# Mixer of a hybrid attention and GLA layer: two heads side by side on halves of TensorE's array, softmax steps over two heads

## The chip, the core and the metric

The kernel runs on one core of a Trainium2 chip. The metric is the device time of one execution in microseconds (us), the median of several runs. A trace of one more execution shows every instruction: on TensorE (PE for matmuls, PEld for loads of the stationary operand), VectorE (DVE), ScalarE (ACT), GpSimd (POOL), and the DMA transfers, which SyncE (SP) issues.

## What is computed

The reference is two layers of a diffusion backbone over 256 tokens of width 1024, with 256 context tokens. The change lies in the mixer of the first layer. It has two branches, whose outputs are laid side by side and projected: windowed attention with 8 query heads on 2 key heads (width 64), and gated linear attention (GLA) in both directions with 4 heads (keys 64 wide, values 128) in chunks of 64 tokens. All of it is float32. Cut to what matters:

```python
def window_attention(q, k, v, kc, vc, sink):
    s_band = jnp.einsum('bnigrd,bnjgd->bgrnij', qb, kb).astype(jnp.float32) * scale
    s_ctx = jnp.einsum('bnigrd,blgd->bgrnil', qb, kc).astype(jnp.float32) * scale
    s_band = jnp.where(valid, s_band, -jnp.inf)
    p = jax.nn.softmax(jnp.concatenate([s_band, s_ctx, sink_l], axis=-1), axis=-1)
    o = (jnp.einsum('bgrnij,bnjgd->bnigrd', p[..., :nk].astype(vb.dtype), vb)
         + jnp.einsum('bgrnil,blgd->bnigrd', p[..., nk:nk + L].astype(vc.dtype), vc))
...
def gla_chunked(q, k, v, log_a, s0):
    q_t = qc_ * jnp.exp(g)
    k_t = kc_ * jnp.exp(-g)
    att = jnp.where(lower, jnp.einsum('bnihd,bnjhd->bnhij', q_t, k_t), 0.0)
    o = jnp.einsum('bnhij,bnjhv->bnihv', att, vc_)
    ...
    o = o + jnp.einsum('bnihd,bnhdv->bnihv', q_t, s_prev)
```

## The kernel before

The program runs in stages, one after the other: the first feed-forward block over tokens and context (two streams), the mixer, a feed-forward block, and the second layer (feed-forward, pooling mixer, feed-forward, final norm). Weights come from HBM through four buffers in `weight` (L138); each is split into a rounded part `hi` on ScalarE (L144) and the rest `lo` on VectorE (L145), and `product` (L322) multiplies a 1024-deep block of weights with the operand in 24 matmuls (L327 to L329).

In the mixer (L705) the projections come one 128-wide block at a time (`project`, L749, in the order of `ORDER`). Small tasks hang on them: rotation of queries and keys (`rope`, L794), transposition of values (`values`, L786), the decay factors of GLA (`gate`, L822), the output gate (`output_gate`, L811). On their results work:

- `scores` (L967): the products of GLA's keys and queries, four heads a block of 128 tokens. `q_t` holds each head in a tile of its own whose other 64 partitions are zero, so that a matmul over all 128 rows (L971) gives one head. A masked copy (L973) writes `att`.
- `states` (L944): the running states `S` of GLA; its matmuls (L951) write the column halves 0 to 63 and 64 to 127 in turn, for two heads.
- `gla_head` (L977): for a head, `att` times values (L984, L991) and `S` times queries (L989) into one bank, then a norm (from L998) with its own small product (L999).
- `attend` (L898): for one query head (j, g) and one block qb of 128 queries: the scores over 256 tokens and 256 context tokens (L904; `k_g` holds each key head with 64 zero partitions), mask and maximum (L907), exponentials (L910, L911), sum and reciprocal (L912, L913), scaling (L914), four transposes (L921), a copy to `PT` (L922), and after the second block the values (L931: four matmuls into one column half of a bank that two heads share). `split` (L892) cuts the result into two parts for the output projection. There are 16 such tasks; three probability buffers (`PBUF`) let three be under way.
- `output` (L1014): the output projection with `merged` (L336, L337), whose first two blocks take up each piece as it is ready.

What is issued when is set by a planner, `Flow` (L63): each task is a generator that gives, step by step, how long TensorE is thought to be busy and what VectorE and ScalarE do after it (`step`, L103); the task of the lowest rank (`RANK`) that is ready by this reckoning is written next. The framework's own scheduler may then shift instructions within an engine. Each engine works through its own list in order; TensorE may start a matmul before earlier ones of another part of its array are through, as the trace shows.

Of the kernel before, what the change touches and what calls it, by code (L numbers as in the profile page):

```python
# [8 lines left out]
F32 = mybir.dt.float32  # L9
# [6 lines left out]
D = 1024  # L16
# [34 lines left out]
PBUF = 3  # L51
# [55 lines left out]
class Body:  # L107
# [597 lines left out]
    def mixer(self, cur, nxt):  # L705
# [12 lines left out]
        k_g = t(lp, [128, 2, 512])  # L718
        k_t = t(lp, [128, 2, 2, T])
        q_t = t(lp, [128, 2, 4, T])  # L720
# [4 lines left out]
        for z in (k_g, q_t, KT):  # L725
            nc.gpsimd.memset(z, 0.0)
# [67 lines left out]
        def rope(blk):  # L794
# [7 lines left out]
            if blk == "ka":  # L802
                for g in (0, 1):
                    r = slice(g * 64, g * 64 + 64)
                    nc.vector.tensor_tensor(k_g[r, g, :T], t1[r], t2[r], op=ALU.add)
                    nc.scalar.copy(k_g[r, g, T:], z[r, T:])
            else:
                nc.vector.tensor_tensor(q_r[:, int(blk[2]), :], t1, t2, op=ALU.add)
# [13 lines left out]
        def gate(d, b):  # L822
# [32 lines left out]
            for hh in (0, 1):  # L855
                r = slice(hh * 64, hh * 64 + 64)
                nc.vector.scalar_tensor_tensor(out=q_t[r, d, 2 * b + hh, :], in0=Z[f"qb{b}"][r], scalar=0.125,
                                               in1=ep[r], op0=ALU.mult, op1=ALU.mult)
# [37 lines left out]
        pv_bank, pv_last, PT = {}, {}, {}  # L896

        def attend(j, g, qb, u):  # L898


            h = g * 4 + j
            sk = self.cols[:, C_SK + h:C_SK + h + 1]
            ps = self.bank()
            nc.tensor.matmul(ps, q_r[:, j, qb * 128:(qb + 1) * 128], k_g[:, g, :], start=True, stop=True)  # L904
            p = t(sp, [128, 512], F32, "P", PBUF)
            st = t(sp, [128, 4], F32, "st", 4)
            nc.vector.tensor_tensor_reduce(out=p, in0=ps, in1=band[:, qb, :], scale=0.125, scalar=sk,  # L907
                                           op0=ALU.add, op1=ALU.max, accum_out=st[:, 0:1])
            nc.vector.tensor_scalar_mul(st[:, 1:2], st[:, 0:1], -1.0)
            nc.scalar.activation(st[:, 3:4], sk, AF.Exp, bias=st[:, 1:2])  # L910
            nc.scalar.activation(p, p, AF.Exp, bias=st[:, 1:2], accum_out=st[:, 2:3])  # L911
            nc.vector.tensor_tensor(st[:, 2:3], st[:, 2:3], st[:, 3:4], op=ALU.add)  # L912
            nc.vector.reciprocal(st[:, 2:3], st[:, 2:3])  # L913
            nc.vector.tensor_scalar_mul(p, p, st[:, 2:3])  # L914
            yield step(0.86, [("D", ATT[0]), ("A", ATT[1]), ("D", ATT[2])])
            if qb == 0:
                PT[h] = t(sp, [128, 4, T], F32, "PT", 2)
            pt = PT[h]
            pk = self.bank()
            for kb in range(4):  # L920
                nc.tensor.transpose(pk[:, kb * 128:(kb + 1) * 128], p[:, kb * 128:(kb + 1) * 128], self.ident)  # L921
            nc.scalar.copy(pt[:, :, qb * 128:(qb + 1) * 128], pk.rearrange("p (k q) -> p k q", q=128))  # L922
            yield step(0.44, [("A", 0.48)], sets=[f"T{u}"])
            if qb == 0:
                return
            if j not in pv_bank:
                pv_bank[j] = self.bank()
            po = pv_bank[j]
            with self.after(pv_last.get(j)):
                for kb in range(4):  # L930
                    ins = nc.tensor.matmul(po[g * 64:(g + 1) * 64, :T], v_sb[:, kb, g * 64:(g + 1) * 64],  # L931
                                           pt[:, kb, :], start=(kb == 0), stop=(kb == 3))
            second = j in pv_last
            pv_last[j] = ins
            if second:
                split(j, po[:, :T])
                yield step(1.72, [("A", 0.31), ("D", 0.34)], sets=[f"a{h}", f"o{j}"])
            else:
                yield step(1.72, sets=[f"a{h}"])
# [27 lines left out]
        def scores(d, tb):  # L967
            ps = self.bank()
            c = slice(tb * 128, (tb + 1) * 128)
            for h in range(4):  # L970
                nc.tensor.matmul(ps[:, h * 128:(h + 1) * 128], k_t[:, d, h // 2, c], q_t[:, d, h, c],  # L971
                                 start=True, stop=True)
            nc.vector.copy_predicated(att[:, d, tb], gm[:, d:d + 1, :].to_broadcast([128, 4, 128]),  # L973
                                      ps.rearrange("p (h i) -> p h i", i=128))
            yield step(0.87, [("D", 0.6)], sets=[f"att{d}{tb}"])

        def gla_head(h):  # L977
            po = self.bank()
            c = slice(h * 128, (h + 1) * 128)
            prev = None  # L980
# [61 lines left out]
        for d in (0, 1):  # L1042
            for tb in (0, 1):
# [244 lines left out]
```

## Time and profile before

| | us |
|---|---|
| three runs | 1159.35, 1162.02, 1163.1 |
| median | 1162.02 |
| the profiled execution | 1161.4 |
| its span, first to last instruction | 1159.2 |
| TensorE busy in the span | 1137.5 |
| VectorE busy | 938.5 |
| ScalarE busy | 587.4 |
| GpSimd busy | 9.9 |

TensorE's clock was granted at 0.997 in the mean. The mixer's scores, states, attention and GLA heads run from about 443 to 546 us of the span; the rest of the output projection follows. Rows of the profile name an instruction by its line in the kernel, its engine, its operation, the tile that it writes and those that it reads, and its shape; `128*64` behind a matmul is the part of the array that it uses (rows times columns). The end of a matmul is modelled, so the distance from one start to the next says more than its busy time. A float32 matmul stands in the trace as two records of a load and a matmul. The order lists of the program count each float32 matmul once.

### The profile page before, as it was taken

To read this page: it belongs to the slowest core of one execution; us is meant where nothing else is said; L and a number is where in the kernel's file an instruction comes from. 1 tells how busy PE (TensorE), PEld (TensorE's weight loads), DVE (VectorE), ACT (ScalarE), POOL (GpSimd) and SP (SyncE) were. 2 spreads that over 40 slices of the span, in tenths; PEclk is the share of its full clock that TensorE was granted. 3 is DMA by queue.
4 is the path that set the end of the run, shared out by engine and by line. 5 is a ranking of instruction groups with operands and counts; after the bars stand their busy time and mean duration, and the time that the engine had idled before them with its cause. 6 is when DMAs were issued, how large, how long until landed. Compare 5 with 4: busy or idle time off the path is not lost.

```text
span 1159.2 us, 19546 instructions
## 1 busy us (share of the span) xinstructions
PE 1137.5 (98%) x7450; PEld 1027.0 (89%) x7450; DVE 938.5 (81%) x1662; ACT 587.4 (51%) x999; POOL 9.9 (1%) x32
## 2 busy tenths in 40 slices
PE   7999999999999999999999999999999999999997
PEld 5899988888888899787999998899999889988886
DVE  6899899787758889776999877989886889967664
ACT  4547645323234474565574444565544556556543
POOL 0000000000000200000000000000000000000000
PEclk9999999999999999999999999999999999999998
DMA  9867557667866535321759977868996864756562
GB/s 332 289 243 240 164 179 233 198 217 243 249 191 191 171 108 177 115 69 54 234 187 324 326 236 246 283 208 284 340 312 203 261 226 147 252 185 192 153 185 88
DMA packets 74544, 247.42 MB, mean 213 GB/s; under 512 B 8273, under 2 KB 8913, under 8 KB 74194
## 3 DMA queue, kind: packets, MB, share of 16 engines
q1 hardware_dynamic: 74450, 246.17, 64.4%
q8 instruction: 58, 0.95, 0.3%
q14 instruction: 36, 0.29, 0.1%
HBM read 245.09 MB, written 1.05 MB: 212 GB/s over the span
## 4 chain that ended last, share of the span: by engine, by line
PE 86%; DVE 7%; DMA 3%; ACT 2%; issue 2%; SPq 0%; DVEq 0%; ACTq 0%
PE t_mm L336 15%; PE t_mm L342 11%; PE t_mm L344 11%; PE t_mm L343 11%; PE t_mm L337 8%; PE t_mm L329 7%; PE t_mm L328 7%; PE t_mm L327 7%; PE t_mm L610 2%; DVE t_lo L145 1%; PE t_mm L931 1%; PE t_mm L904 1%; DVE t_junk L174 1%; DMA t_x<-ctxT 1%; ACT t_hi L144 1%
## 5 line engine op out<-in xcount | busy, mean ns | idle before, releaser
L144 ACT CAST t_hi<-t_raw 128x1024 fp32r<-128x1024 f32 (+1 forms) x344 | 326.0, 950 | 368.2 <-PE t_mm L343 160.8
L145 DVE TENSOR_TENSOR t_lo<-t_raw,t_hi 128x1024 fp32r<-128x1024 f32 (+1 forms) x344 | 376.6, 1097 | 87.2 <-ACT t_hi L144 84.1
L327 PE MATMUL t_mm<-t_xA,t_hi 128*128 128x258 f32 (+1 forms) x912 | 261.0, 287 | 2.7 <-DVE t_x L957 1.6
L329 PE MATMUL t_mm<-t_xA,t_lo 128*128 128x258 f32 (+1 forms) x912 | 259.6, 285 | 3.1 <-DVE t_lo L145 3.1
L328 PE MATMUL t_mm<-t_xA,t_hi 128*128 128x258 f32 (+1 forms) x912 | 258.1, 283 | 0.1
L174 DVE CUSTOM_DVE_ANT_0 t_junk<-t_rawm,t_x 128x1024 bf16<-128x1024 f32 x142 | 181.7, 1280 | 23.8 <-DMA t_rawm<-wmod 22.9
L336 PE MATMUL t_mm<-t_g,t_hi 128*128 128x512 f32 x528 | 186.6, 398 | 0.0
L344 PE MATMUL t_mm<-t_xA,t_lo 128*128 128x256 f32 (+1 forms) x592 | 186.2, 315 | 0.0
L342 PE MATMUL t_mm<-t_xA,t_hi 128*128 128x256 f32 (+1 forms) x592 | 186.2, 315 | 0.0
L343 PE MATMUL t_mm<-t_xA,t_hi 128*128 128x256 f32 (+1 forms) x592 | 186.2, 315 | 0.0
L327 PEld LDWEIGHTS t_mm<-t_xA,t_hi 128*128 128x128 f32 x912 | 173.0, 190 | 5.9 <-DVE t_x L957 1.9
L329 PEld LDWEIGHTS t_mm<-t_xA,t_lo 128*128 128x128 f32 x912 | 172.6, 189 | 4.2 <-DVE t_lo L145 4.2
L328 PEld LDWEIGHTS t_mm<-t_xA,t_hi 128*128 128x128 f32 x912 | 172.7, 189 | 2.4 <-issue 1.4
L337 PE MATMUL t_mm<-t_g,t_lo 128*128 128x256 f32 x528 | 147.9, 280 | 0.0
L336 PEld LDWEIGHTS t_mm<-t_g,t_hi 128*128 128x128 f32 x528 | 99.2, 188 | 23.8
L343 PEld LDWEIGHTS t_mm<-t_xA,t_hi 128*128 128x128 f32 x592 | 112.9, 191 | 6.9
L344 PEld LDWEIGHTS t_mm<-t_xA,t_lo 128*128 128x128 f32 x592 | 112.9, 191 | 6.9
L342 PEld LDWEIGHTS t_mm<-t_xA,t_hi 128*128 128x128 f32 x592 | 112.9, 191 | 6.7
L337 PEld LDWEIGHTS t_mm<-t_g,t_lo 128*128 128x128 f32 x528 | 99.7, 189 | 0.0
L336 PE MATMUL t_mm<-t_xA,t_hi 128*128 128x512 f32 x272 | 95.4, 396 | 0.0
L337 PE MATMUL t_mm<-t_xA,t_lo 128*128 128x256 f32 x272 | 75.4, 278 | 0.0
L342 PE MATMUL t_mm<-t_g,t_hi 128*128 128x512 f32 x176 | 68.5, 389 | 0.0
(244 smaller groups left out, 1388.7 us busy)
## 6 DMA issues: line engine op xcount, KB each, us to landing
t_raw<-wi SPq DMA_DIRECT2D x190, 512.0 KB, 4.6
t_rawm<-wmod SPq DMA_DIRECT2D x118, 512.0 KB, 4.5
t_raw<-wo SPq DMA_DIRECT2D x64, 384.0 KB, 3.6
t_raw<-wo SPq DMA_DIRECT2D x64, 320.0 KB, 3.3
t_raw<-win SPq DMA_DIRECT2D x18, 512.0 KB, 3.7
t_w<-wmod SPq DMA_DIRECT2D x16, 512.0 KB, 6.6
t_raw<-wmod SPq DMA_DIRECT2D x10, 512.0 KB, 4.3
t_raw<-wi0k SPq DMA_DIRECT2D x8, 512.0 KB, 6.3
```

The costliest lines, as they stand in the source:

```text
L144: nc.scalar.copy(hi[:, :n], raw[:, :n])
L145: self.mark = nc.vector.tensor_tensor(lo[:, :n], raw[:, :n], hi.bitcast(F32)[:, :n], op=ALU.subtract)
L174: self.nc.vector.tensor_tensor_reduce(out=junk, in0=w, in1=self.srow[s], scale=0.5 if half else 1.0, scalar=b, op0=ALU.mult, op1=ALU.add, ...
L327: nc.tensor.matmul(ps[:, :n], hi[:, c], X[:, 0, k, :n], start=(k == 0), stop=False)
L328: nc.tensor.matmul(ps[:, :n], hi[:, c], X[:, 1, k, :n], start=False, stop=False)
L329: nc.tensor.matmul(ps[:, :n], lo[:, c], X[:, 0, k, :n], start=False, stop=(k == KB - 1))
L336: nc.tensor.matmul(ps, hi, X.rearrange("p x t -> p (x t)"), start=first, stop=False)
L337: nc.tensor.matmul(ps[:, T:], lo, X[:, 0], start=False, stop=last)
L342: nc.tensor.matmul(ps, hi, X0, start=first, stop=False)
L343: nc.tensor.matmul(ps, hi, X1, start=False, stop=False)
L344: nc.tensor.matmul(ps, lo, X0, start=False, stop=last)
L610: nc.tensor.matmul(ps[i][:, :T], w[:, i * 128:(i + 1) * 128], xf[:, k, :], start=(k == 0), stop=(k == KB - 1))
```

## The change

Heads are taken in pairs, one on each half of the partitions. `q_t` and `k_g` lose their zero-padded copies: each holds two heads on partitions 0 to 63 and 64 to 127, and a matmul reads 64 partitions (`rows(g)`), which places it on one half of the array's rows. Two such matmuls for two heads stand next to each other and write two banks of PSUM.

- `attend` handles both key heads g for a (j, qb): 8 tasks in place of 16. It issues two score matmuls, two mask-and-maximum steps, one negation over two columns, the exponentials of both heads, one sum, one reciprocal, two scalings, eight transposes and two copies. The values of both heads are written in turn to the two column halves, in one visit in place of two. Four probability buffers in place of three hold two pairs; the two `PT` buffers now hold one pair.
- `scores` handles a direction at a time, 8 matmuls in pairs, with two masked copies in place of two a call before (four in all, as before).
- `gla_head` multiplies `S` and queries on the 64 rows of its head.
- `gate` and `rope` fill the tiles in one step over 128 partitions in place of two over 64, and two clearings on GpSimd go.
- The planner's figures for these steps are set anew (`SC`, `PVT`).

Lines after L50 stand one lower in the changed file, and later ones shift by a few: L904 is L904 in both, L907 becomes L908, L921 L924, L931 L932, L951 L947, L971 L970, L984 to L991 become L986 to L993, L999 becomes L1001.

```diff
-PBUF = 3
+PBUF = 4
+SC, PVT = 0.9, 1.0
...
-        k_g = t(lp, [128, 2, 512])
+        k_g = t(lp, [128, 512])
...
-        q_t = t(lp, [128, 2, 4, T])
+        q_t = t(lp, [128, 2, 2, T])
...
-        for z in (k_g, q_t, KT):
-            nc.gpsimd.memset(z, 0.0)
+        nc.gpsimd.memset(KT, 0.0)
...
-                for g in (0, 1):
-                    r = slice(g * 64, g * 64 + 64)
-                    nc.vector.tensor_tensor(k_g[r, g, :T], t1[r], t2[r], op=ALU.add)
-                    nc.scalar.copy(k_g[r, g, T:], z[r, T:])
+                nc.vector.tensor_tensor(k_g[:, :T], t1, t2, op=ALU.add)
+                nc.scalar.copy(k_g[:, T:], z[:, T:])
...
-            for hh in (0, 1):
-                r = slice(hh * 64, hh * 64 + 64)
-                nc.vector.scalar_tensor_tensor(out=q_t[r, d, 2 * b + hh, :], in0=Z[f"qb{b}"][r], scalar=0.125,
-                                               in1=ep[r], op0=ALU.mult, op1=ALU.mult)
+            nc.vector.scalar_tensor_tensor(out=q_t[:, d, b, :], in0=Z[f"qb{b}"], scalar=0.125, in1=ep,
+                                           op0=ALU.mult, op1=ALU.mult)
...
+        def rows(g):
+            return slice(g * 64, g * 64 + 64)
+
+        def attend(j, qb, u):
+            sk = [self.cols[:, C_SK + g * 4 + j:C_SK + g * 4 + j + 1] for g in (0, 1)]
+            ps = [self.bank() for _ in (0, 1)]
+            for g in (0, 1):
+                nc.tensor.matmul(ps[g], q_r[rows(g), j, qb * 128:(qb + 1) * 128], k_g[rows(g), :], start=True, stop=True)
+            P = [t(sp, [128, 512], F32, "P", PBUF) for _ in (0, 1)]
+            st = t(sp, [128, 4, 2], F32, "st", 2)
+            for g in (0, 1):
+                nc.vector.tensor_tensor_reduce(out=P[g], in0=ps[g], in1=band[:, qb, :], scale=0.125, scalar=sk[g],
+                                               op0=ALU.add, op1=ALU.max, accum_out=st[:, 0, g:g + 1])
+            nc.vector.tensor_scalar_mul(st[:, 1, :], st[:, 0, :], -1.0)
+            for g in (0, 1):
+                nc.scalar.activation(st[:, 3, g:g + 1], sk[g], AF.Exp, bias=st[:, 1, g:g + 1])
+                nc.scalar.activation(P[g], P[g], AF.Exp, bias=st[:, 1, g:g + 1], accum_out=st[:, 2, g:g + 1])
+            nc.vector.tensor_tensor(st[:, 2, :], st[:, 2, :], st[:, 3, :], op=ALU.add)
+            nc.vector.reciprocal(st[:, 2, :], st[:, 2, :])
+            for g in (0, 1):
+                nc.vector.tensor_scalar_mul(P[g], P[g], st[:, 2, g:g + 1])
+            yield step(SC, [("D", 2 * ATT[0]), ("A", 2 * ATT[1]), ("D", 2 * ATT[2])])
...
+            po = self.bank()
+            for kb in range(4):
+                for g in (0, 1):
+                    nc.tensor.matmul(po[rows(g), :T], v_sb[:, kb, rows(g)], PT[j][g][:, kb, :],
+                                     start=(kb == 0), stop=(kb == 3))
+            split(j, po[:, :T])
+            yield step(PVT, [("A", 0.4), ("D", 0.42)], sets=[f"o{j}"])
...
+        def scores(d):
+            ps = [self.bank() for _ in (0, 1)]
+            for i, (tb, b) in enumerate(((0, 0), (0, 1), (1, 0), (1, 1))):
+                c = slice(tb * 128, (tb + 1) * 128)
+                for hh in (0, 1):
+                    nc.tensor.matmul(ps[hh][:, i * 128:(i + 1) * 128], k_t[rows(hh), d, b, c], q_t[rows(hh), d, b, c],
+                                     start=True, stop=True)
+            for hh in (0, 1):
+                nc.vector.copy_predicated(att[:, d, :, hh::2, :],
+                                          gm[:, d:d + 1, :].unsqueeze(1).to_broadcast([128, 2, 2, 128]),
+                                          ps[hh].rearrange("p (t b i) -> p t b i", t=2, b=2))
+            yield step(SC, [("D", 1.4)], sets=[f"att{d}"])
...
-                            nc.tensor.matmul(po[:, cc], S[:, d, ch, h // 2, :], q_t[:, d, h, cc],
+                            nc.tensor.matmul(po[:, cc], S[r, d, ch, h // 2, :], q_t[r, d, h // 2, cc],
...
-            need = ["tka", "tva", f"tqa{j}"] + ([f"T{u - PBUF}"] if u >= PBUF else [])
-            flow.add(RANK["attend"], attend(j, g, qb, u), need)
+            need = ["tka", "tva", f"tqa{j}"] + ([f"T{u - PBUF // 2}"] if u >= PBUF // 2 else [])
+            flow.add(RANK["attend"], attend(j, qb, u), need)
```

More of the change, by code (lines that the diff above doesn't have):

```diff
@@ L894, in split @@
             nc.vector.tensor_tensor(O[:, k, 1], src, O.bitcast(F32)[:, k, 0], op=ALU.subtract)
[L896 to L915, printed above, removed]
-            if qb == 0:
[L917 to L923, printed above, removed]
@@ new lines, in rows @@
+        def rows(g):
+            return slice(g * 64, g * 64 + 64)
+        PT = {}
+        def attend(j, qb, u):
[17 more added lines that the diff above has]
+            yield step(SC, [("D", 2 * ATT[0]), ("A", 2 * ATT[1]), ("D", 2 * ATT[2])])
+            if qb == 0:
+                PT[j] = [t(sp, [128, 4, T], F32, "PT", 2) for _ in (0, 1)]
+            for g in (0, 1):
+                pk = self.bank()
+                for kb in range(4):
+                    nc.tensor.transpose(pk[:, kb * 128:(kb + 1) * 128], P[g][:, kb * 128:(kb + 1) * 128], self.ident)
+                nc.scalar.copy(PT[j][g][:, :, qb * 128:(qb + 1) * 128], pk.rearrange("p (k q) -> p k q", q=128))
+            yield step(0.88, [("A", 1.1)], sets=[f"T{u}"])
@@ L924, in attend @@
             if qb == 0:
                 return
[L926 to L939, printed above, removed]
+            po = self.bank()
+            for kb in range(4):
+                for g in (0, 1):
+                    nc.tensor.matmul(po[rows(g), :T], v_sb[:, kb, rows(g)], PT[j][g][:, kb, :],
+                                     start=(kb == 0), stop=(kb == 3))
+            split(j, po[:, :T])
@@ L965, in states @@
             yield step(1.08, [("D", 1.2)], sets=[f"S{d}{b}"])
[L967 to L975, printed above, removed]
+        def scores(d):
[10 more added lines that the diff above has]
+            yield step(SC, [("D", 1.4)], sets=[f"att{d}"])
         def gla_head(h):
@@ L979, in gla_head @@
             c = slice(h * 128, (h + 1) * 128)
+            r = rows(h % 2)
             prev = None
@@ L1042, in mixer @@
         for d in (0, 1):
-            for tb in (0, 1):
-                flow.add(RANK["scores"], scores(d, tb), [f"qk{d}0", f"qk{d}1"])
+            flow.add(RANK["scores"], scores(d), [f"qk{d}0", f"qk{d}1"])
         for d in (0, 1):
@@ L1048, in mixer @@
         for h in range(4):
-            flow.add(RANK["gla"], gla_head(h), [f"S{d}{h // 2}" for d in (0, 1)] + [f"att{d}{tb}" for d in (0, 1) for tb in (0, 1)]
+            flow.add(RANK["gla"], gla_head(h), [f"S{d}{h // 2}" for d in (0, 1)] + [f"att{d}" for d in (0, 1)]
                      + [f"sr{h}"])
-        seq = [(j, g, qb) for j in range(4) for g in (0, 1) for qb in (0, 1)]
-        for u, (j, g, qb) in enumerate(seq):
-            need = ["tka", "tva", f"tqa{j}"] + ([f"T{u - PBUF}"] if u >= PBUF else [])
-            flow.add(RANK["attend"], attend(j, g, qb, u), need)
+        for u, (j, qb) in enumerate((j, qb) for j in range(4) for qb in (0, 1)):
+            need = ["tka", "tva", f"tqa{j}"] + ([f"T{u - PBUF // 2}"] if u >= PBUF // 2 else [])
+            flow.add(RANK["attend"], attend(j, qb, u), need)
         flow.add(RANK["output"], output(), ["rb3"])
```

## The prediction, made before the changed kernel ran

> **What bounds the kernel now.** I read the page first, for the shares of the span:
>
> ```profile
> span 1159.2 us, 19546 instructions
> PE 1137.5 (98%) x7450; PEld 1027.0 (89%) x7450; DVE 938.5 (81%) x1662; ACT 587.4 (51%) x999; POOL 9.9 (1%) x32
> ```
>
> TensorE is the bound on average, but the change lives in one stage. So I cut the mixer's part of the span into stretches (us, then busy time and instructions of each engine, granted clock, DMA share, GB/s): scores and gates, attention beside the projections, attention's tail, output projection.
>
> ```profile
> 443.00:460.00 17.00, 16.32 (x158) 15.74 (x156) 14.70 (x28) 7.90 (x14) 1.44 (x1) 1.00 0.69 231
> 460.00:500.00 40.00, 39.04 (x268) 30.82 (x269) 31.07 (x91) 21.93 (x48) 0.00 (x0) 1.00 0.37 117
> 500.00:546.50 46.50, 46.50 (x297) 36.61 (x295) 31.47 (x95) 25.99 (x65) 0.15 (x2) 1.00 0.12 41
> 546.50:568.00 21.50, 21.05 (x127) 18.55 (x127) 18.82 (x38) 14.70 (x26) 0.00 (x0) 1.00 0.65 220
> ```
>
> From 443 to 546 TensorE has almost no hole, VectorE is busy 77.2 of 103.5, ScalarE 55.8, the clock is full, the DMA queues are slack. The one real wait of TensorE there is this:
>
> ```profile
> 460.96 0.39 PE L327 MATMUL t_mm<-t_xA,t_hi 128*128 128x258 f32 x1 [1.64 <-DVE t_x L957]
> ```
>
> A us that TensorE no longer needs in this stage comes off the end, as long as nothing new makes it wait. So the question is what the matmuls cost, and what is late next.
>
> **The change, part by part.** For the costs I read TensorE in order of time (start, us, engine, line, tile). A busy time overlaps with the next one's, so I count from start to start:
>
> ```profile
> 443.25 0.60 PE L790 MATMUL t_mm<-t_x,t_z 128*128 128x128 f32 x4
> 443.69 3.74 PE L971 MATMUL t_mm<-t_x 128*128 128x128 f32 x32
> 447.18 0.36 PE L327 MATMUL t_mm<-t_xA,t_hi 128*128 128x258 f32 x1
> ...
> 477.39 0.60 PE L790 MATMUL t_mm<-t_x,t_z 128*128 128x128 f32 x4
> 477.93 1.94 PE L931 MATMUL t_mm<-t_PT,t_x 128*64 128x256 f32 x8
> 479.80 2.84 PE L904 MATMUL t_mm<-t_x 128*128 128x512 f32 x6
> 482.57 2.40 PE L951 MATMUL t_mm<-t_x 128*64 128x128 f32 x40
> 484.90 0.66 PE L921 MATMUL t_mm<-t_x,t_P 128*128 128x128 f32 x4
> 485.54 0.39 PE L327 MATMUL t_mm<-t_xA,t_hi 128*128 128x258 f32 x1
> ...
> 505.37 0.60 PE L921 MATMUL t_mm<-t_x,t_P 128*128 128x128 f32 x4
> 505.81 1.02 PE L904 MATMUL t_mm<-t_x 128*128 128x512 f32 x2
> ...
> 516.02 1.88 PE L904 MATMUL t_mm<-t_x 128*128 128x512 f32 x4
> 517.34 0.68 PE L327 MATMUL t_mm<-t_xA,t_hi 128*128 128x258 f32 x1
> ...
> 520.65 0.59 PE L999 MATMUL t_mm<-t_osq,t_x 128*128 128x256 f32 x2
> 521.17 1.94 PE L931 MATMUL t_mm<-t_PT,t_x 128*64 128x256 f32 x8
> ```
>
> An fp32 product stands as two records (x32 for the 16 products of L971). The GLA scores take 3.49 us, 0.109 a record. The states of L951 stream the same 128 columns, 40 records in 2.33 us: 0.058 a record. They write column halves 0 and 64 in turn. That two halves really run side by side is seen in the first 0.05 us of each group (second number: TensorE, with the records under way):
>
> ```profile
> 443.68:443.73 0.05, 0.04 (x1) 0.05 (x2) 1.00 0.00 0
> ...
> 456.90:456.95 0.05, 0.04 (x2) 0.04 (x2) 1.00 0.34 82
> ```
>
> One record of L971, two of L951. So alternating halves cost one stream for two products.
>
> *Values (L931).* The chain of waits gives a visit and the scores (start, us):
>
> ```profile
> 495.79 1.87 PE t_mm L931 x8
> ...
> 498.25 1.72 PE t_mm L904 x4
> ```
>
> Eight visits, each in one column half, cost 8 x 1.87 = 15.0 us. Afterwards four visits hold both heads in alternating halves, each as long as one is now: 7.5. Saves 7.5. This is the overlap that L951 shows, so I take it whole; if nothing overlapped it would be 0.
>
> *Attention scores (L904).* 32 records at 0.43 are 13.8 us. Two heads on row halves 0 and 64, each with its own PSUM bank, need 6.9. Saves 6.9. No row shows row halves; the nearest is L951's column halves, which overlap fully. Bounds 0 and 6.9; I take 6.9.
>
> *GLA scores (L971).* 3.49 becomes 1.75 by the same step. Saves 1.75, bounds 0 and 1.75.
>
> [...]
>
> *Switches of shape.* L790's four transposes take 0.54 before L931 and 0.44 before L971: entering a half-array group costs 0.10. Four transposes behind L951 take 0.64, at 505.37 they take 0.44: leaving costs up to 0.20. The program now has 10 half-array visits, 20 changes. After the change I count 34, because the four products of the GLA state (L989 now) shrink to one row half between full-array ones, twice in each of four heads (16 changes), while scores and values often stand back to back. 14 more at 0.2 are 2.8 us. Bounds: 14 x 0.1 = 1.4, and twice 2.8 if row halves drain longer.
>
> This is TensorE where the first values stand, before (t_PT the transposed probabilities, t_P the probabilities):
>
> ```order
> L790 MATMUL t_mm<-t_x,t_z_4595 128x128 x4
> L931 MATMUL t_mm<-t_PT,t_x 64x256 x4
> L904 MATMUL t_mm<-t_x 128x512 x3
> L951 MATMUL t_mm<-t_x 64x128 x20
> L921 MATMUL t_mm<-t_x,t_P 128x128 x4
> ```
>
> and after it:
>
> ```order
> L790 MATMUL t_mm<-t_x,t_z_4590 128x128 x4
> L932 MATMUL t_mm<-t_PT,t_x 64x256 x8
> L904 MATMUL t_mm<-t_x 128x512 x4
> L947 MATMUL t_mm<-t_x 64x128 x20
> L328 MATMUL t_mm<-t_xA,t_hi 128x258
> ```
>
> One visit now holds the values of two heads (x8), the scores come in fours (two blocks of two heads), and the transposes move behind the next projection.
>
> *Softmax in pairs.* One head's chain at the end of the stage, VectorE and then ScalarE:
>
> ```profile
> 539.93 0.75 DVE L907 CUSTOM_DVE_ANT_0 t_P<-t_mm,t_x 128x512 f32<-128x512 f32 x1 [1.33 <-PE t_mm L904]
> 540.61 0.08 DVE L907 DVE_READ_ACCUMULATOR2_ANT t_st<- 128x1 f32 x1
> 540.73 0.15 DVE L909 TENSOR_SCALAR t_st<-t_st 128x1 f32<-128x1 f32 x1
> ...
> 541.95 0.16 DVE L912 TENSOR_TENSOR t_st<-t_st 128x1 f32<-128x1 f32 x1
> ...
> 542.34 0.49 DVE L914 TENSOR_SCALAR t_P<-t_P,t_st 128x512 f32<-128x512 f32 x1
> ```
> ```profile
> 540.91 0.29 ACT L910 ACTIVATE t_st<-t_x,t_st 128x1 f32<-128x1 f32 x1 [2.80 <-DVE t_st L909]
> 541.12 0.71 ACT L911 ACTIVATE t_P<-t_P,t_st 128x512 f32<-128x512 f32 x1
> ...
> 541.82 0.56 ACT L922 COPY t_PT<-t_mm 128x512 f32<-128x512 f32 x1
> ```
>
> The big steps stay one per head; only L909, L912 and L913 halve in number, 24 small steps of 0.07 to 0.2 that lie beside TensorE. Worth nothing here. But four heads are now queued at once, and the transposes wait for the last. Where is TensorE's cover too short? In the first three rounds 5 to 8 us of projection, states or GLA head lie between. In the last round it stands so, after the change (L986 to L993 a GLA head, L1001 its norm):
>
> ```order
> L986 MATMUL t_mm<-t_x 128x128
> L991 MATMUL t_mm<-t_x 128x64 x4
> L993 MATMUL t_mm<-t_x 128x128
> L932 MATMUL t_mm<-t_PT,t_x 64x256 x8
> L904 MATMUL t_mm<-t_x 128x512 x4
> L328 MATMUL t_mm<-t_xA,t_hi 128x258
> ...
> L330 MATMUL t_mm<-t_xA,t_lo 128x258
> L1001 MATMUL t_mm<-t_osq,t_x 128x256
> L924 MATMUL t_mm<-t_x,t_P 128x128 x16
> ```
>
> where before stood, at the last projection:
>
> ```order
> L931 MATMUL t_mm<-t_PT,t_x 64x256 x4
> L921 MATMUL t_mm<-t_x,t_P 128x128 x4
> L904 MATMUL t_mm<-t_x 128x512 x2
> L327 MATMUL t_mm<-t_xA,t_hi 128x258
> ...
> L329 MATMUL t_mm<-t_xA,t_lo 128x258
> L999 MATMUL t_mm<-t_osq,t_x 128x256
> L931 MATMUL t_mm<-t_PT,t_x 64x256 x4
> ```
>
> What moved: the transposes of these scores stood after another values visit; now all sixteen follow one projection and the small norm product. TensorE gets there in 521.17 - 516.02 = 5.15 plus a switch, 5.3 us after its first score, and needs 16 x 0.11 = 1.8, so it would be through at 7.1. VectorE starts 1.06 after the scores start (538.87 to 539.93 in the row before; I take 1.1), does three L907 at 0.68 and L909 (0.12), ScalarE starts 0.18 later and takes 0.91 for each of four exponentials (540.91 to 541.82): 3.6; then 0.13 to L912, 0.39 to L914, and two of those, 0.9. That is 1.1 + 2.0 + 0.3 + 3.6 + 1.4 = 8.4, and the last four transposes end at 8.9. TensorE waits 1.8 us, a wait that the trace does not have now. Bounds 0 (VectorE earlier) and 3.5 (VectorE still busy with an earlier head).
>
> *Tail.* The last GLA head now ends the stage, and its norm product follows at once:
>
> ```profile
> L994 ACT ACTIVATE t_osq<-t_mm x4: 384/384/391, 505.6 to 537.4; 128x256 f32<-128x256 f32 x4
> ```
>
> 0.38 of square and some 0.2 of hand-over are bare: 0.6 us. The long chain behind it is covered by output blocks that stand between.
>
> *Edits ahead of the scores.* One full-height step replaces two of 64 partitions:
>
> ```profile
> L857 DVE SCALAR_TENSOR_TENSOR t_x<-t_qb,t_gp 64x256 f32<-64x256 f32 x8 | 3.3, 416 | 0.1
> L805 DVE TENSOR_TENSOR t_x<-t_rp,t_rp 64x256 f32<-64x256 f32 x2 | 0.8, 417 | 0.0
> ```
>
> Four and one are left, 2.1 us less on VectorE, which TensorE waits for at 460.96. But TensorE arrives there 1.75 earlier too, so the 1.64 stays about as it is: 0, bounds -1.6 and +1.7. The dropped clearings on GpSimd wait for nobody: 0. The masked copies keep their number and size: 0. No DMA is added, removed or moved past another in SP's queue; the fourth probability buffer costs only memory.
>
> *Behind the stage.* From 546.5 VectorE is busy 18.8 of 21.5 us, TensorE 21.05. Both keep their work, so the saving passes on: 0, at worst +1 us.
>
> Sum: -7.5 - 6.9 - 1.75 + 2.8 + 1.8 + 0.6 = -10.95, say -11.0. The profiled execution took 1161.4 us, 2.2 around its span of 1159.2; it becomes 1150.4. The median of the runs, 1162.0, lies 0.6 higher, so I forecast 1151.0.
>
> **The rivals.**
> *Row halves do not overlap* (0.12). Column halves are shown, row halves by no row, and their stationary loads are 128 wide (L971) and not 64. Then 8.65 of the gain is gone; the scores take longer, which swallows the last round's wait of 1.8: -11.0 + 8.65 - 1.8 = -4.1, 1157.9.
>
> *A product finishes both passes first* (0.08). A pair A, B then needs three slots (A1, A2 with B1, B2). Four score groups, four values visits and the GLA scores each lose one slot: 4 x 0.43 + 4 x 0.23 + 0.11 = 2.7, so 1153.7. Two records within 0.05 us at 456.90 speak against it. [...]
>
> *Slower: TensorE starves on the paired softmax* (0.05). If VectorE's and ScalarE's queues, with the projections' steps among them, are late in all four rounds, each round waits up to 8.4 less 1.7 of scores and 1.3 of earlier transposes, 5.4: +21.6 against a gain of 7.5 + 6.9 + 1.75 - 2.8 - 0.6 = 12.75, so +8.9, 1170.9. It decides at 12.75/4 = 3.2 us a round. VectorE's 23% of free time and 5 us of cover speak against it.
>
> *Nothing overlaps* (0.04), the alternating halves of L931's shape and the rows alike run one after the other: only the switches stay, +2.8, 1164.8.
>
> **How the numbers follow.** The forecast has the remaining 0.71. Its own bounds, by the switches (-1.4, +2.8), the last round (-1.8, +1.7) and the edits ahead (-1.6, +1.7), not all at one end, are 1147 to 1155. The range must reach into the first rival to leave out no more than 2 in 10: 1147 to 1158.5. A measurement tells 0.3%, 3.5 us, from no change. Faster: forecast, second rival and over half of the first, 0.85; within 0.3%: the rest of the first and most of "nothing overlaps", 0.09; slower 0.06.
>
> **What would show it.** Right: the GLA scores start two records within 0.05 us and take about 1.75 us; four score products take 1.7; a values visit of 16 records stays near 1.9; the sixteen last transposes show a hole of about 1.8 us with a wait for VectorE; the mixer ends near 535.5 in place of 546.5. Wrong: 0.11 a record still in the GLA scores (rows do not overlap); holes before transposes in several rounds (starved); GLA heads (L984 to L991 now) that take much longer than before (switches dearer, or loads no longer hidden); a later stage that waits for VectorE by what TensorE gained.

## The result, and the profile after

The changed kernel takes 1152.9 us (median of 4 runs, 1150.8 to 1153.9), the kernel before in the runs beside it 1162.4: a ratio of 0.9926, 95% interval 0.991 to 0.9941, so 6.9 to 10.5 us less. The forecast was 1151.0, eleven us less. A second series of the changed kernel gave 1153.4 and 0.993 (0.9917 to 0.9942), 6.7 to 9.6 us less.

The page of the profiled execution (1152.8 us, its span 1151.0) shows the same number of matmuls, with less time in them:

```profile
span 1151.0 us, 19523 instructions
PE 1126.8 (98%) x7450; PEld 1020.5 (89%) x7450; DVE 932.8 (81%) x1633; ACT 585.5 (51%) x998; POOL 7.3 (1%) x30
```

Two profiled executions also differ where the kernels don't: the first GLA score starts at 443.69 us before and at 441.84 after, and TensorE had those 1.9 us already at 85 us, in code that is the same. From that first score on to the end of the span there are 715.5 us before and 709.2 after. So 6.4 us is what the traces of one execution each have to explain; the medians say 9.5 in the first series and 8.1 by the second's ratio.

TensorE in order of time in the changed kernel (L970 GLA scores, L932 values, L904 attention scores, L986 to L993 a block of a GLA head):

```profile
441.84 2.06 PE L970 MATMUL t_mm<-t_x 64*128 64x128 f32 x32
443.83 0.39 PE L328 MATMUL t_mm<-t_xA,t_hi 128*128 128x258 f32 x1
...
457.68 0.39 PE L328 MATMUL t_mm<-t_xA,t_hi 128*128 128x258 f32 x1 [1.69 <-DVE t_x L953]
...
474.67 1.95 PE L932 MATMUL t_mm<-t_PT,t_x 128*64 128x256 f32 x16
476.55 1.99 PE L904 MATMUL t_mm<-t_x 64*128 64x512 f32 x8
478.46 1.75 PE L947 MATMUL t_mm<-t_x 128*64 128x128 f32 x28
...
496.08 0.38 PE L986 MATMUL t_mm<-t_x 128*128 128x128 f32 x2
496.39 1.10 PE L991 MATMUL t_mm<-t_x 64*128 64x64 f32 x8
497.42 0.49 PE L993 MATMUL t_mm<-t_x 128*128 128x128 f32 x2
497.75 0.39 PE L986 MATMUL t_mm<-t_x 128*128 128x128 f32 x2
...
516.60 1.06 PE L924 MATMUL t_mm<-t_x,t_P 128*128 128x128 f32 x8 [0.85 <-DVE t_P L917]
518.42 1.09 PE L924 MATMUL t_mm<-t_x,t_P 128*128 128x128 f32 x8 [0.75 <-DVE t_P L917]
...
532.69 1.12 PE L1001 MATMUL t_mm<-t_osq,t_x 128*128 128x256 f32 x2 [0.47 <-ACT t_osq L996]
```

From start to start: the 32 records of GLA scores take 1.99 us (3.49 before), sixteen records of values 1.88, eight of attention scores 1.91, with 0.2 of shape change in each group of scores. Both kinds of halves run side by side. Within a group of attention scores the pairs of records follow at 0.43 us, which was the step of one record before; the 0.2 lies at its two ends. The first wait, behind the states, stands as it did. The holes before the sixteen transposes are new, and so is the one before the last norm.

A block of a GLA head before, for comparison:

```profile
502.69 0.39 PE L984 MATMUL t_mm<-t_x 128*128 128x128 f32 x2
502.91 1.00 PE L989 MATMUL t_mm<-t_x 128*128 128x64 f32 x8
503.75 0.44 PE L991 MATMUL t_mm<-t_x 128*128 128x128 f32 x2
504.03 0.39 PE L984 MATMUL t_mm<-t_x 128*128 128x128 f32 x2
```

1.34 us a block before, 1.67 now: two changes of shape cost 0.33, and eight blocks 2.65.

What the forecast had nothing for shows in the stretches of the last norm (columns as in the prediction; the granted clock is the third from the end):

```profile
530.00:532.50 2.50, 2.22 (x16) 1.78 (x14) 1.70 (x4) 0.59 (x2) 0.00 (x0) 1.00 0.00 0
532.50:533.00 0.50, 0.31 (x1) 0.31 (x2) 0.33 (x1) 0.43 (x2) 0.00 (x0) 0.84 0.00 0
533.00:536.00 3.00, 3.00 (x10) 2.44 (x10) 1.55 (x5) 0.83 (x2) 0.00 (x0) 0.50 0.84 309
536.00:536.50 0.50, 0.50 (x4) 0.46 (x4) 0.47 (x2) 0.00 (x0) 0.00 (x0) 0.75 0.56 229
536.50:540.00 3.50, 3.50 (x22) 3.06 (x22) 1.18 (x4) 0.75 (x2) 0.00 (x0) 1.00 0.28 70
```

For 3.41 us (0.16 of the half microsecond at 0.84, three whole, and half of the one at 0.75) TensorE ran at half its clock: ten matmuls in 3 us where 19 go into 3 us behind it. That costs 1.7 us. Before, no stretch up to the last matmuls had it.

The table of TensorE's waits from 450 to 640 us (us in all, times, the longest), after and then before:

```profile
PE t_mm L328 <- DVE t_x L953: 1.7, 1, 1.7
PE t_mm L330 <- DVE t_lo L146: 1.7, 3, 0.8
PE t_mm L924 <- DVE t_P L917: 1.6, 2, 0.9
PE t_mm L1001 <- ACT t_osq L996: 0.5, 1, 0.5
PE t_mm L338 <- DVE t_lo L146: 0.3, 1, 0.3
```
```profile
PE t_mm L327 <- DVE t_x L957: 1.6, 1, 1.6
PE t_mm L329 <- DVE t_lo L145: 0.8, 2, 0.4
```

Behind the stage TensorE waits 2.0 us (L330 and L338) for the low halves of weights that VectorE subtracts, in place of 0.8. Counted from start to start beyond the usual step of each line, the loss behind 538 us is 3.7 in place of 2.0 behind 547, up to 640 us.

### The profile page after: what moved, and what is told of

Read it like the earlier page. It is cut to its first block, busy times and chain, and to the rows that moved or that the text cites. A ratio compares the mean times of both kernels' runs of the same rounds, so it can differ in the third digit from the quotient of the medians.

```text
span 1151.0 us, 19523 instructions
## 1 busy us (share of the span) xinstructions
PE 1126.8 (98%) x7450; PEld 1020.5 (89%) x7450; DVE 932.8 (81%) x1633; ACT 585.5 (51%) x998; POOL 7.3 (1%) x30
## 4 chain that ended last, share of the span: by engine, by line
PE 85%; DVE 8%; DMA 3%; ACT 2%; issue 1%; SPq 0%; DVEq 0%; ACTq 0%
PE t_mm L337 15%; PE t_mm L344 11%; PE t_mm L345 11%; PE t_mm L343 11%; PE t_mm L338 8%; PE t_mm L330 7%; PE t_mm L329 7%; PE t_mm L328 7%; PE t_mm L611 2%; DVE t_lo L146 2%; DVE t_junk L175 1%; ACT t_hi L145 1%; PE t_mm L991 1%; DMA t_raw<-wi0k 1%; PE t_mm L932 1%
## 5 line engine op out<-in xcount | busy, mean ns | idle before, releaser
L330 PE MATMUL t_mm<-t_xA,t_lo 128*128 128x258 f32 (+1 forms) x912 | 259.7, 285 | 3.8 <-DVE t_lo L146 3.7
L328 PE MATMUL t_mm<-t_xA,t_hi 128*128 128x258 f32 (+1 forms) x912 | 260.0, 286 | 2.8 <-DVE t_x L953 1.7
L328 PEld LDWEIGHTS t_mm<-t_xA,t_hi 128*128 128x128 f32 x912 | 173.0, 190 | 7.4 <-DVE t_x L953 1.9
L330 PEld LDWEIGHTS t_mm<-t_xA,t_lo 128*128 128x128 f32 x912 | 172.7, 189 | 5.1 <-DVE t_lo L146 5.1
L338 PE MATMUL t_mm<-t_g,t_lo 128*128 128x256 f32 x528 | 148.1, 280 | 0.0
L338 PEld LDWEIGHTS t_mm<-t_g,t_lo 128*128 128x128 f32 x528 | 99.7, 189 | 0.0
L338 PE MATMUL t_mm<-t_xA,t_lo 128*128 128x256 f32 x272 | 75.7, 280 | 0.3 <-DVE t_lo L146 0.3
```

The lines of the kernel that those rows point to most:

```text
L328: nc.tensor.matmul(ps[:, :n], hi[:, c], X[:, 0, k, :n], start=(k == 0), stop=False)
L330: nc.tensor.matmul(ps[:, :n], lo[:, c], X[:, 0, k, :n], start=False, stop=(k == KB - 1))
L338: nc.tensor.matmul(ps[:, T:], lo, X[:, 0], start=False, stop=last)
```

## The experiments

Theory at the outset: the side-by-side halves save what was forecast; changes of shape, two waits and the stretch of half clock take some back. Rivals: the gain comes from fewer and longer steps and not from halves side by side; or what TensorE gains it waits for behind the stage. Each run's time stands with its ratio to the kernel before in the same runs; 0.0025 is 2.9 us. The start of the mixer scatters from 441.2 to 444.8 us, and the half clock comes and goes, so this table has from each trace the time from the first GLA score to the end, against 715.5 before, and where the clock was at half ahead of the last matmuls:

| kernel | against before, us | half clock, us of the span |
|---|---|---|
| before | 0 | nowhere |
| changed | -6.4 | 532.8 to 536.3 |
| changed, again | -6.1 | 532.6 to 536.1 |
| values apart | -2.5 | 539.4 to 542.8 |
| attention scores full | -1.8 | 459.6 to 463.0 |
| states full | -7.7 | 458.2 to 461.7 |
| last round filled | -6.4 | 458.6 to 462.0, 543.9 to 550.7 |
| paired heads | -7.4 | 498.9 to 502.4, 536.5 to 539.9 |
| state steps apart | -9.3 | nowhere |
| values by twos | -8.3 | nowhere |
| states full, steps apart | -10.6 | nowhere |
| paired heads as cover | -12.8 | nowhere |
| changed, weights split on GpSimd | -1.9 | 563.1 to 566.5 |
| cover, weights split on GpSimd | -7.2 | 558.7 to 562.1 |

**Values apart.** Does TensorE need the halves to alternate in the queue?

```diff
-            for kb in range(4):
-                for g in (0, 1):
+            for g in (0, 1):
+                for kb in range(4):
                     nc.tensor.matmul(po[rows(g), :T], v_sb[:, kb, rows(g)], PT[j][g][:, kb, :],
```

> The changed kernel with the four products of one head's values ahead of the four of the other, in place of alternating column halves; nothing else differs. Theory (the halves run side by side only because neighbours in the queue sit in different halves): a visit of 16 records takes 3.7 us in place of 1.87, four visits cost 7.5 us more, 1152.9 becomes 1160.4. Rival 1 (TensorE finds the free half by itself, eight records deep): a visit stays near 1.9 us and the time at 1152.9. Rival 2 (the gain came from fewer, longer visits and softmax steps for two heads, not from side by side): the visit is 3.7 us, but the waits behind it shrink by as much, and the time stays within 2 us of 1152.9.

1155.7 us, 0.9953 (0.9941 to 0.9966): 2.9 us slower than the changed kernel by ratio, between the theory and the first rival, and more than the 2 us that the second allows. A visit in the trace:

```profile
477.59 2.86 PE L932 MATMUL t_mm<-t_PT,t_x 128*64 128x256 f32 x16
480.38 1.99 PE L904 MATMUL t_mm<-t_x 64*128 64x512 f32 x8
```

It takes 2.79 us, neither 1.87 nor 3.74. The second head's first record starts 0.92 us into the visit, beside the first head's fifth, though the kernel writes all eight of the first head ahead of it: the two ran side by side for about half of each one's time. (The trace shows when records start, not their order in the queue.)

**Values by twos.** The same with two products of one head, then two of the other.

```diff
-            for kb in range(4):
-                for g in (0, 1):
+            for kb, g in ((0, 0), (1, 0), (0, 1), (1, 1), (2, 0), (3, 0), (2, 1), (3, 1)):
```

> The changed kernel with the values products in the order two of one head, two of the other, and so on. With all four of a head first, the second head's began beside the first's after half of it, four records, and a visit took 2.8 us where 1.87 is full overlap and 3.74 is none. Theory (TensorE starts a product ahead of others if its half is free and it stands within about four records): two and two still overlap in full but for the start, visits of 1.9 to 2.3 us. Rival (the second half starts only where the first reaches the half of its own chain): again three quarters, 2.8 us.

One run, 1152.0 us. The visit:

```profile
475.73 2.00 PE L931 MATMUL t_mm<-t_PT,t_x 128*64 128x256 f32 x16
477.66 1.99 PE L904 MATMUL t_mm<-t_x 64*128 64x512 f32 x8
```

1.93 us, where strict alternation took 1.88: it isn't needed on the column halves. The theory holds in this one order; that some four records are the reach is the author's estimate from these two visits, 2.79 us by fours and 1.93 by twos.

**Attention scores full.** The zero rows of the keys are back, for this one product.

```diff
-                nc.tensor.matmul(ps[g], q_r[rows(g), j, ...], k_g[rows(g), :], start=True, stop=True)
+                nc.tensor.matmul(ps[g], q_r[:, j, ...], k_g[:, g, :], start=True, stop=True)
```

> The changed kernel with the attention scores on the full array again, the key rows of the other head zero, as before the change; values, GLA scores, paired softmax stay. Theory (row halves overlap in full): a group of four products takes 3.44 us in place of 1.8, four groups cost 6.6 us more. In the last round the softmax starts earlier against the transposes, so the wait of 1.93 us before them shrinks to about 0.3, and if the half-rate clock at 532.8 to 536.3 us follows from the waits, its 1.7 us go too: 1152.9 + 6.6 - 1.6 - (0 to 1.7), 1156 to 1158. Rival (the row halves are worth less than that, because the scores already ran beside the next projection's first loads): under 3 us more, below 1155.

1158.7 us, 0.9967 (0.9956 to 0.9979): 4.5 us slower by ratio. A group of eight records, up to the next line:

```profile
480.53 3.70 PE L907 MATMUL t_mm<-t_x 128*128 128x512 f32 x8
484.16 1.09 PE L950 MATMUL t_mm<-t_x 128*64 128x128 f32 x16
```

3.63 us in place of 1.91. Row halves overlap in full, and the rival of a small gain falls. Where a projection follows, its first record starts beside the last score; counted up to its second, the four groups cost 6.2 us more. The wait before the last transposes shrinks from 1.6 to 0.6, and the half clock stands at another place for the same price. That makes 5.2, where the times show 4.5 and the traces 4.6.

**States full.** The query tile has its zero rows again, and L991 runs on the full array.

```diff
-                            nc.tensor.matmul(po[:, cc], S[r, d, ch, h // 2, :], q_t[r, d, h // 2, cc],
+                            nc.tensor.matmul(po[:, cc], S[:, d, ch, h // 2, :], q_t[:, d, h, cc],
```

> The changed kernel with the four state products of each block of a GLA head on the full array again (the query rows of the other head zero), as before the change; GLA scores, attention scores and values keep their halves. Theory (16 more changes of array shape cost the heads 3.2 us): the four heads take 10.8 us on TensorE in place of 14.0, 1152.9 becomes 1149.7. A second question is the half-rate clock at the end of the stage, 1.7 us: if it comes from half-empty array use in the heads, it goes here too, 1148.0; if it comes from TensorE's waits of 1.93 and 0.8 us, which stay here, it stays. Rival (a half-height product is itself slower, or the price of a change of shape hides behind weight loads): the heads stay at 14.0 us and the time at 1152.9.

1150.5 us, 0.9901 (0.9887 to 0.9916): 3 us faster than the changed kernel, its interval just below that of the second series and overlapping that of the first by a little. A block:

```profile
498.18 0.39 PE L989 MATMUL t_mm<-t_x 128*128 128x128 f32 x2
498.40 1.00 PE L994 MATMUL t_mm<-t_x 128*128 128x64 f32 x8
499.24 0.44 PE L996 MATMUL t_mm<-t_x 128*128 128x128 f32 x2
499.52 0.39 PE L989 MATMUL t_mm<-t_x 128*128 128x128 f32 x2
```

1.34 us again. The half-height state products gained nothing and cost sixteen changes of shape, 2.65 us. The trace is only 1.3 to 1.6 us shorter, since ahead of the heads TensorE waits 1.0 us more in it (0.51 at 443.91, and 2.16 in place of 1.69 behind the states). The half clock is not bound to half-height heads: here it stands behind the first wait, from 458.2.

**Last round filled.** The third head and output blocks go between the last projection and the sixteen transposes.

```diff
-            yield step(1.75, [("A", GL)])
+            yield step(1.75, sets=[f"g{h}"])
+            yield step(0.0, [("A", GL)])
...
-            yield step(SC, [("D", 2 * ATT[0]), ("A", 2 * ATT[1]), ("D", 2 * ATT[2])])
+            yield step(SC, [("D", 2 * ATT[0]), ("A", 2 * ATT[1]), ("D", 2 * ATT[2])],
+                       needs=["g2"] if j == 3 else [])
```

> The changed kernel with the third GLA head and two output blocks put between the last projection and the sixteen last transposes; the last head then has output blocks behind it too. The same instructions in another order at the end of the stage. Theory (waits and the clock cost what they show): the wait of 1.93 us and the tail's 0.8 us go, and with them the half-rate clock, 1.7 us: 1152.9 becomes 1148.5, and the granted clock is 1.00 from 443 us to the end of the stage. Rival 1 (the waits go, but the half-rate clock comes from half-height work in the heads, and stays): 1150.2. Rival 2 (what TensorE gains here it waits for VectorE's weight split right behind the stage): 1152 to 1153.5, with holes before L328 to L338 grown by some 3 us.

1152.5 us, 0.992 (0.9907 to 0.9932): not to be told from the changed kernel. The waits before the transposes and at the last norm are gone from the table; that behind the states (L328) stays, and another is new:

```profile
PE t_mm L337 <- ACT t_hi L145: 2.0, 2, 1.9
PE t_mm L328 <- DVE t_x L954: 1.9, 1, 1.9
```

```profile
541.00:544.00 3.00, 1.15 (x6) 0.61 (x5) 2.81 (x8) 3.00 (x7) 0.00 (x0) 0.98 0.72 284
544.00:550.60 6.60, 6.45 (x19) 4.96 (x20) 5.18 (x9) 2.50 (x6) 0.00 (x0) 0.50 0.43 141
```

TensorE reaches the output projection's next weights before ScalarE, busy in all of 541 to 544, has copied them, and waits 1.9 us; behind that wait the clock is at half for 6.8 us, which costs 3.4. The second rival holds in time and in kind: the wait moved behind the stage, though to ScalarE's copy and not to VectorE's subtraction, and a half clock stands behind it.

**Paired heads.** Two heads in one step; their state products alternate between row halves. In this kernel the second block's accumulation starts while the first one's is open in the same bank, and its result lacks part of the sum (relative error 0.326); the engines' work is the same.

```diff
+            for d in (0, 1):
+                for ch in range(4):
+                    cc = slice(ch * CHUNK, (ch + 1) * CHUNK)
+                    for hh in (0, 1):
+                        nc.tensor.matmul(po[hh][:, cc], S[rows(hh), d, ch, b, :], q_t[rows(hh), d, b, cc],
+                                         start=False, stop=False, skip_group_check=True)
```

> The changed kernel with two GLA heads in one step: the eight products of both on the full array stand together, the state products of the two heads alternate between the row halves, square and norm cover both heads on 512 columns, and output blocks stand ahead of the last sixteen transposes. Theory: a pair of heads takes 32 x 0.112 / 2 + 32 x 0.056 + 2 changes of shape, 4.0 us, so both pairs 8.0 us in place of 14.0; the last round's wait of 1.9 and the tail's 0.8 are covered: 1152.9 - 6.0 - 2.7 = 1144.2, and 1142.5 without a half-rate clock. Rival 1 (behind the stage the weight split of VectorE takes back what TensorE gains): the stage is 8 us shorter, but holes before the next weights grow by 5 us, and the time is about 1149. Rival 2 (products of 64 columns are bound by their weight loads, which the row halves do not share): the state products stay at 0.112 a record, the pairs take 11.5 us, 1148.

1152.6 us, 0.9919 (0.9905 to 0.9932). The pair itself does what was expected, 32 state records in 1.93 us:

```profile
504.27 1.05 PE L984 MATMUL t_mm<-t_x 128*128 128x128 f32 x8
505.26 2.00 PE L990 MATMUL t_mm<-t_x 64*128 64x64 f32 x32
507.19 1.16 PE L994 MATMUL t_mm<-t_x 128*128 128x128 f32 x8
```

But a longer step needs a longer cover. From the table of waits:

```profile
PE t_mm L337 <- DVE t_xA L890: 3.9, 2, 2.5
PE t_mm L328 <- DVE t_x L954: 1.8, 1, 1.8
PE t_mm L925 <- DVE t_P L917: 1.7, 2, 1.0
```

The output blocks wait 3.9 us for VectorE's last step on their inputs (L890), the third round's transposes 1.7 for the softmax that a head had covered, and the clock was at half twice, which costs 3.4. Neither stated rival holds: the records take 0.06 us, and what took the gain back is not the weight split.

**State steps apart.** The second of two state steps waits in the plan for the first, and a projection comes between.

```diff
-            flow.add(RANK["states"], states(d, b), [f"kt{d}{b}", f"tvb{2 * b}", f"tvb{2 * b + 1}"])
+            flow.add(RANK["states"], states(d, b), [f"kt{d}{b}", f"tvb{2 * b}", f"tvb{2 * b + 1}"]
+                     + ([f"S0{b}"] if d else []))
```

> The changed kernel with the two state steps that stood back to back (L947, twenty products, eight PSUM banks) kept apart by a projection; behind them TensorE waits 1.9 us for VectorE (L953) to empty the first bank. Theory (the wait is for the bank, and VectorE has time for it one projection later): the wait at 455.7 us goes, two visits more cost four changes of shape, 0.6 us: 1152.9 - 1.9 + 0.6 = 1151.6. Rival (VectorE is simply behind at that place after the gates): the wait shows up at the next product that needs VectorE, 1153.5.

1152.0 us, 0.9918 (0.9902 to 0.9933), 1.2 us less by ratio, though the intervals overlap. In the trace the wait is gone but for 0.3 us and no half clock follows: -9.3 in place of -6.4 and -6.1. This fits the theory: the wait was for a bank that VectorE had time to empty later.

**The changed kernel again.** Nothing altered: do the waits and the half clock come at the same places?

> The changed kernel once more, nothing altered. TensorE's waits should recur: 1.9 us behind the first states, 1.9 us before the sixteen last transposes, 0.5 and 0.3 us at the last norm. [...]

1153.4 us, 0.993 (0.9917 to 0.9942). The waits recur, and the half clock stands at the same place, at the last norm; in values apart, too, it stands there (539.4). But the same work with values by twos, and the same waits, has no half clock:

```profile
530.00:540.00 10.00, 9.53 (x59) 8.15 (x58) 6.19 (x16) 3.38 (x8) 0.00 (x0) 1.00 0.32 109
```

59 matmuls stand in these ten us where the changed kernel has at most 16 + 1 + 10 + 4 + 22 = 53, and that trace is 1.9 to 2.2 us shorter behind the first score (-8.3 against -6.4 and -6.1), with visits 0.06 us longer each. So the half clock costs some 2 us where it falls, and the head's work alone doesn't bring it.

The traces show when it comes, and not what brings it. Each stretch lasts 3.4 us (3.41 in the changed kernel) but for the one of 6.8; in the changed kernel the clock is at half once more behind the last matmul, from 1147.24 us. Where one trace has two starts ahead of the last matmuls, they lie 37.55 us apart (paired heads, 498.94 and 536.49) and 85.3 (last round filled), 11.0 and 25.0 times 3.41. In the 3.41 us ahead of a start TensorE was busy for 0.28 to 0.49 of the time in eight of the table's eleven cases. This is the stretch ahead of 459.63 in attention scores full (behind its bounds come its length and TensorE's busy time):

```profile
456.22:459.63 3.41, 1.50 (x20) 1.26 (x17) 2.61 (x7) 1.18 (x2) 0.00 (x0) 1.00 0.70 199
```

In the other three it was busy for 0.86, 0.99 and 0.86, all at the last norm. In the second trace of the changed kernel:

```profile
529.22:532.64 3.42, 3.39 (x25) 2.82 (x23) 2.33 (x6) 0.83 (x2) 0.00 (x0) 1.00 0.00 0
```

TensorE was busy for 3.39 of 3.42 us there, with the last head, and the wait for the norm began only at 532.61, so no long wait stands ahead of this half clock; its cause stays open. Behind the states it came at the end of a wait of 2.16 us (states full), or within 0.8 us behind one of 1.91 (attention scores full) and one of 1.9 (last round filled). It did not come there after 1.64 (before), 1.69 (changed) or 1.8 (the changed kernel's second trace, and paired heads, where TensorE was busy for 0.47 of the 3.41 us from 454.6).

**Both small repairs.** States full, and state steps apart.

> Two edits on the changed kernel: the state products of the GLA heads on the full array again (alone 2.9 us less), and the two state steps kept apart by a projection (alone 1.4 us less). Theory (they remove different things: sixteen changes of shape, and a wait for a PSUM bank): the gains add, 1153.4 - 2.9 - 1.4 = 1149.1. Rival (both gained mainly by sparing the half-rate clock, which can be spared once): 1150.5.

1151.3 us, 0.9903 (0.9888 to 0.9918): no better than states full alone (0.9901). That is the rival's number but not its reason, for the trace of states full has the half clock, and so its gain did not come from sparing it; and this trace shows the best of the small repairs, -10.6. Whether they add in the median is open.

**Paired heads as cover.** Each pair stands between a round's scores and its transposes; `rb0` to `rb3` come earlier, norms are per head, the state steps are apart, and only the first product of a bank starts an accumulation.

```diff
-ORDER = "kb0 qb1 zg qb0 kb1 ka va vb0 vb1 qa0 vb2 qa1 vb3 qa2 rb0 rb1 qa3 rb2 rb3".split()
+ORDER = "kb0 qb1 zg qb0 kb1 ka va vb0 vb1 qa0 vb2 qa1 vb3 rb0 rb1 qa2 rb2 rb3 qa3".split()
...
+            flow.add(RANK["gla"], gla_pair(b), [f"S{d}{b}" for d in (0, 1)] + [f"att{d}" for d in (0, 1)]
+                     + [f"sr{2 * b}", f"sr{2 * b + 1}", f"tqa{2 + b}"])
```

> The changed kernel with two GLA heads in one step (row halves for their state products), each pair placed between the scores of the third and the fourth round and their transposes, the state steps kept apart, the gate projections rb0 to rb3 earlier, the norms per head. Theory (the pair saves 5.7 us on TensorE and now stands where the paired softmax needs cover): both pairs 8.3 us in place of 14.0; the waits of 1.9 (states), 1.9 (last transposes) and 0.8 (last norm) go, the half-rate clock (1.7) with them, four more changes of shape cost 0.6: 1153.4 - 5.7 - 4.6 - 1.7 + 0.6 = 1142. Rival 1 (the output projection behind waits for VectorE's last norms and weight splits): the stage is 11 us shorter, but 4 us come back as holes behind it, 1146. Rival 2 (as with the pair in its first place, holes before the transposes and the half-rate clock take it all): 1151 to 1153.

1147.7 us, 0.9874 (0.9857 to 0.989): the best of all, 14.7 us below before and 6.3 below the changed kernel by ratio. The last round:

```profile
513.99 1.99 PE L904 MATMUL t_mm<-t_x 64*128 64x512 f32 x8
515.91 1.16 PE L983 MATMUL t_mm<-t_x 128*128 128x128 f32 x8
517.00 2.00 PE L989 MATMUL t_mm<-t_x 64*128 64x64 f32 x32
...
522.02 1.98 PE L924 MATMUL t_mm<-t_x,t_P 128*128 128x128 f32 x16
```

8.03 us lie between the first score and the transposes, which now wait for nothing; in the changed kernel TensorE got there after 5.5 (510.25 to 516.60, less the 0.85 of the wait). The theory's 1142 is missed by 5.7, and the first rival's 1146 lies nearest: waits of 1.2 us are left in the second round, and 2.7 behind the stage, where that rival put 4.

**Weights split on GpSimd.** To find what takes time back behind the stage, GpSimd subtracts the first four low halves there, once in the changed kernel and once in paired heads as cover.

```diff
+        if self.spare > 0:
+            self.spare -= 1
+            nc.gpsimd.tensor_tensor(lo[:, :n], raw[:, :n], hi.bitcast(F32)[:, :n], op=ALU.subtract)
```

> The changed kernel with the low halves of the first four weights behind the output projection subtracted by GpSimd, which is idle there, in place of VectorE; the rest is as it was. Asked is what takes back some 1.8 us behind the stage. Theory (VectorE's queue: the subtractions stand behind residual and normalisation steps, 0.9 us of TensorE's wait at 554.6 and 0.6 at 558.3): the two waits shrink by 1 to 1.5 us together, 1153.4 becomes 1152.2. Rival 1 (the weights themselves come late, SP and ScalarE's copies pace them): the waits stay, 1153.4. Rival 2 (GpSimd takes so much longer for a subtraction than VectorE's 1.2 us that TensorE waits for it): longer waits, 1155 or more.

> The kernel with paired GLA heads as cover (1147.7 alone) with the same four subtractions on GpSimd; behind its stage TensorE waits 1.2 and 0.6 us for VectorE's low halves. Theory: these waits go, 1146.3. Rival 1 (the weights come late): 1147.7. Rival 2 (GpSimd is too slow): 1150 or more.

1158.7 us, 0.9975 (0.9965 to 0.9986), and 1152.6, 0.9927 (0.9915 to 0.9939): 5 and 6 us worse than without. GpSimd in the first of them, from 530 to 600 us:

```profile
L149 POOL TENSOR_TENSOR t_lo<-t_raw,t_hi 128x1024 fp32r<-128x1024 f32 x4 | 10.2, 2568 | 33.3 <-ACT t_hi L146 30.4 <-DVE t_x L355 2.9
```

2.57 us for what VectorE does in 1.2, and TensorE waits 5.8 us behind the stage in the first of the two, in place of 2.0. The second rival holds, and the cause of the loss behind the stage stays open.

## Why the prediction was nearly right

*Values, 7.5 less.* Right: eight visits of 1.87 became four of 1.88.

*Attention scores, 6.9 less.* Right in kind: 32 x 0.43 = 13.8 became 4 x 1.91 = 7.6, so 6.1, with the 0.2 of shape change in each group. Full overlap of row halves was taken without a row that showed it, a bet that came in; the full-array run confirms it. With the GLA scores the row pairs saved 7.6 of the forecast 8.65.

*GLA scores, 1.75 less.* 1.5, again with the change of shape. The rival that a product finishes both passes first is refuted by the 1.91, which leaves no third slot.

*Changes of shape, 2.8 more.* The counts of 20 and 34 are those of the traces. The heads alone took 2.65; the ten changes of the scores' groups are in the two terms above. The states-full run shows that this term bought nothing: the state products could have stayed at full height.

*The last round, 1.8.* 1.6 in the table of waits, 1.9 from start to start, where forecast and with the releaser forecast. *The tail, 0.6:* 0.5. *Edits ahead, 0:* the 1.64 became 1.69.

*What failed* is the step "Behind the stage": it was costed at 0, at worst +1, and 1.7 was lost there (3.7 for 2.0). And the half clock at the last norm, 1.7 us, was in no term; the trace of before has it nowhere ahead of the last matmuls and could not show it. With both, -7.5 - 6.1 - 1.5 + 2.65 + 1.9 + 0.5 + 1.7 + 1.7 is -6.65. Matched matmul by matmul from the first GLA score on, the two traces are 8.5 us apart at 542.5 us of the changed kernel, 6.8 at 635.2, where this sum ends, and 6.4 at the end of the span; the last 0.4 went in code that is the same.

That the medians differ by 9.5 and the traces by 6.4 is not settled. The intervals of the two ratios reach down to 6.9 and 6.7 us; there is one trace of before, and its execution may have been a good one. By the terms as the traces have them the time would have been 1155.4, so that the forecast lies within 2 us of the median is in part luck.

## What to carry to other kernels

Small products paired up here on halves of the array at 1.75 to 2 times the rate, on rows (32 records of GLA scores in 1.99 us for 3.49) and on columns (the values of two heads in 1.88 us for twice 1.87), with partners that stood near in the order written: by fours the values took 2.79. But half-height state products alone between full-height ones saved nothing and paid 0.16 us a change. Pairing also lengthened the step behind (1.6 us of wait before the last transposes), since two heads queue for VectorE and ScalarE, so place the cover first: paired heads were worth 1 us in the old place, and 6 once they stood where the softmax needed them, with the state steps apart (alone worth 1.2). And a wait of TensorE can cost more than its length: behind the states the half clock, some 1.7 us each time, came with the three waits of 1.9 us and more and with none of 1.8 or less, though the traces don't show what brings it.

## Unexpected in the hardware

- The clock at half came in nine of thirteen traces of the changed kernel and its variants, for 3.4 us each time and once for 6.8; it cost 1.7 to 3.4 us. Eight of its eleven starts follow 3.41 us in which TensorE was busy for 0.28 to 0.49, three follow 0.86 to 0.99. Equal work with equal waits had it (changed kernel) or not (values by twos).
- With all four products of one head's values written first, the second head's started 0.92 us into the visit, beside the first head's fifth record, and the visit took 2.79 us; by twos it took 1.93.
- State products of 64 columns take 0.11 us a record alone (8 in 0.84 before) and 0.06 in row pairs (32 in 1.93).
- GpSimd took 2.57 us for a subtraction of 128x1024 that VectorE does in 1.22.
